# The first work of a hybrid decoder block: value projection of the undilated heads ahead of the state-space inputs, on raw x

## The chip, the cores and the metric

The kernel runs on one core of a Trainium2 chip. The metric is the device time of one execution in microseconds. The shapes are one batch of 512 tokens by 1024 model channels, in float32.

## The reference, cut to what matters

One decoder layer:

- `h = RMSNorm(x)`: every token's row is divided by its root mean square, and every channel is multiplied by `norm_w`.
- `proj = h @ w_in`, whose columns are split into `u` and `z` of a state-space branch (1024 columns each), queries, keys and values of three head groups (512 columns each per group), a gate `z_a` (512) and two merge gates `r_s`, `r_a` (1024 each).
- State-space branch: with `lam`, `dt`, `b` a diagonal complex recurrence over the tokens is run for 64 groups of 16 channels with 64 states, and read out with `c`; then GELU, a gated unit with `w_glu`, a SiLU gate and `w_ssm_out`.
- Attention branch: three head groups with window and dilation (128, 1), (512, 4) and (2048, 16). The values of the first group, which is not dilated, are the ones that this change moves. Then a SiLU gate and `w_attn_out`.
- The branches are gated, summed, multiplied by `w_o` and added to x.

Since the root mean square is one number per token, a projection can be made of raw x times `norm_w`, and its rows be divided by the root afterwards.

## The kernel before, in words

Every float32 product is made of three passes of a reduced float32 type: both operands are split into a high part (ScalarE, a copy that rounds) and a low part (VectorE, the difference), and TensorE adds high x high, high x low and low x high. So each weight block of 128x1024 costs one `w_hi` instruction on ScalarE (line 248) and one `w_lo` on VectorE (line 250), and `h` is split in the same way into `hT_hi` (line 349) and `hT_lo` (line 351), held transposed: channels on partitions, in eight slices k of 128, tokens along the free side.

A projection is made in one of two ways. Channel-major (`cm_unit`): 128 columns of the weights are the stationary side and all 512 tokens stream, 24 products (8 slices by 3 passes) of 512 columns. Token-major (`wide_granule`): 128 tokens of `h` are stationary and 512 columns of the weights stream, 96 products for 512 columns.

TensorE's instructions stand in the order of the code: each is issued behind the one before (`pe`, `follow`). In the first part of the kernel ScalarE's and VectorE's are pinned too, by `on_act` and `on_dve`. What goes through neither, as all work of GpSimd and the loads on SyncE's queue, is put in order by a planner when the program is built, by its own estimate of when each instruction can start. The engines and queues then work in that order and wait where an input is late.

The start: x is loaded in three parts (tokens are dealt so that row r of `x_all` holds tokens r, r+4, ...), with weights between them. TensorE warms up with 38 transposes of a unit matrix. The first half (rows 0 and 1) is squared and summed on ScalarE and VectorE (`square`, `square_dve`), `inverse_rms` makes the inverse root `rst`, `scale_dve` and `scale_act` multiply x by it in place, and `h_turn` turns the 16 blocks of 128x128 on TensorE into PSUM (`hps`). `h_split` multiplies by `norm_w` (`nwc`) and splits. `first_pass` then makes u0, u1 and u2, the first 384 channels of `u`, over the first 256 tokens, while the second half of x goes the same way; then over the second 256 tokens.

Behind it the coefficients of the recurrence are made from `lam` and `dt` on VectorE, with two sines on ScalarE (`sincos`); `f_turn` turns them on TensorE (`ftp`). The projections u3 to u7, `z_a`, `z`, `r_s`, the undilated values (`v0_granule`, 96 products) and a granule with other values follow as filler units. Events, given in blocks of six products of these units, hang the state-space work between them: `W0` the first input coefficients (`wps`), `K0B` the first output kernels, `Y0` the first read-out (`yps`). The recurrence itself (`step`, lines 753 to 758) runs on VectorE beside them. `d_load` loads the skip weights and multiplies them on GpSimd (line 812).

The values go through ScalarE (`act.copy`) into `vt` and from there to memory (`vd`), from which `v0_load` brings them back in the order of the attention.

## Time and profile before

| | |
|---|---|
| time, median of 3 runs | 668.4 us (668.23 to 668.57) |
| profiled execution, its own time | 668.63 us |
| its span | 666.7 us |
| TensorE busy | 660.2 us, 4617 products and transposes |
| VectorE busy | 466.2 us |
| ScalarE busy | 321.0 us |
| GpSimd busy | 116.8 us |
| granted TensorE clock over the span | 1.0 |

PE is TensorE, PEld its weight load, DVE VectorE, ACT ScalarE, POOL GpSimd, SP SyncE; a q behind a name is the engine's queue of issues. A row of the timeline gives start, length, engine, line, operation, out<-in, shapes and a count, and in brackets the idle time of the engine before it and what ended that. A row of the groups gives busy time, mean ns of one, and the idle time of the engine before. A row of the chain of waits gives start, length and what the end of the kernel hung on then. Products are pipelined, so their own lengths overlap; the distance between starts is what one costs.

### The profile page before, as it was taken

What the parts mean: (1) busy time and instruction counts of PE and PEld (TensorE: products, weight loads), DVE (VectorE), ACT (ScalarE), POOL (GpSimd) and SP (SyncE); (2) the same over time, 40 slices, a digit from 0 to 9 for tenths busy, and PEclk for the clock granted to TensorE, in tenths of its full rate; (3) what the DMA queues carried; (4) which work ended last, traced back from release to release, by engine and by line L of the source; (5) the groups of instructions that cost most, each with busy time, mean ns of one, the idle gap of its engine ahead of it and who ended that gap; (6) DMA issues with size and microseconds to landing.
All of it is one profiled execution on the core that took longest, in us unless ns stands there. A gap on an engine that the chain in (4) does not pass through costs nothing.

```text
span 666.7 us, 12357 instructions
## 1 busy us (share of the span) xinstructions
PE 660.2 (99%) x4617; PEld 553.7 (83%) x4617; DVE 466.2 (70%) x965; ACT 321.0 (48%) x676; POOL 116.8 (18%) x274
## 2 busy tenths in 40 slices
PE   8999999999999999999999999999999999999998
PEld 7988888888888888888888888888888888888887
DVE  7898989999786469833238676758575957657531
ACT  6636444432667545422444664557356645633210
POOL 1010000600375257600000030022002200210000
PEclk9999999999999999999999999999999999999999
DMA  9646364744666644564244223222232314347231
GB/s 310 128 126 178 85 189 132 183 140 130 169 151 154 156 139 142 165 207 118 64 126 128 80 63 112 64 77 83 80 94 64 96 50 126 104 139 277 94 127 63
DMA packets 137618, 85.25 MB, mean 128 GB/s; under 512 B 33104, under 2 KB 124248, under 8 KB 137304
## 3 DMA queue, kind: packets, MB, share of 16 engines
q1 hardware_dynamic: 135352, 81.98, 41.6%
q0 software_dynamic: 2048, 2.36, 2.4%
q8 instruction: 36, 0.59, 0.4%
q14 instruction: 22, 0.18, 0.1%
q10 hardware_dynamic: 160, 0.14, 0.1%
HBM read 70.03 MB, written 12.06 MB: 123 GB/s over the span
## 4 chain that ended last, share of the span: by engine, by line
PE 96%; DVE 1%; DMA 1%; issue 1%; ACT 0%; ACTq 0%
PE pj L69 81%; PE sps L69 3%; PE yps L69 3%; PE ot L69 2%; PE ptp L74 2%; PE qtp L74 2%; PE xps L69 1%; PE wps L74 1%; DMA x_all<-in_x_dram 1%; PE kps L69 1%; PE yT L74 1%; ACT w_hi L248 0%; DVE hT_lo L351 0%; PE hps L74 0%; PE cps L74 0%
## 5 line engine op out<-in xcount | busy, mean ns | idle before, releaser
L248 ACT ACTIVATE w_hi<-w_raw 128x1024 fp32r<-128x1024 f32 x94 | 99.3, 1059 | 169.1 <-PE pj L69 121.2
L250 DVE TENSOR_TENSOR w_lo<-w_raw,w_hi 128x1024 fp32r<-128x1024 f32 x94 | 118.9, 1266 | 66.0 <-ACT w_hi L248 65.5
L69 PE MATMUL pj<-hT_hi,w_hi 128*128 128x512 f32 (+1 forms) x312 | 119.0, 383 | 0.0
L69 PE MATMUL pj<-hT_lo,w_hi 128*128 128x512 f32 (+1 forms) x312 | 116.3, 375 | 0.4 <-DVE hT_lo L351 0.4
L69 PE MATMUL pj<-w_hi,hT_hi 128*128 128x512 f32 x288 | 115.2, 400 | 0.0
L69 PE MATMUL pj<-hT_hi,w_lo 128*128 128x512 f32 (+1 forms) x312 | 114.4, 374 | 0.0
L69 PE MATMUL pj<-w_hi,hT_lo 128*128 128x512 f32 x288 | 112.4, 390 | 0.0
L69 PE MATMUL pj<-w_lo,hT_hi 128*128 128x512 f32 x288 | 112.3, 390 | 0.0
L69 PEld LDWEIGHTS pj<-hT_hi,w_hi 128*128 128x128 f32 x312 | 59.1, 189 | 9.7
L69 PEld LDWEIGHTS pj<-hT_lo,w_hi 128*128 128x128 f32 x312 | 58.9, 189 | 9.9 <-DVE hT_lo L351 0.6
L69 PEld LDWEIGHTS pj<-hT_hi,w_lo 128*128 128x128 f32 x312 | 57.7, 188 | 10.7
L69 PEld LDWEIGHTS pj<-w_hi,hT_lo 128*128 128x128 f32 x288 | 54.0, 188 | 11.7
L69 PEld LDWEIGHTS pj<-w_hi,hT_hi 128*128 128x128 f32 x288 | 54.1, 188 | 10.5
L69 PEld LDWEIGHTS pj<-w_lo,hT_hi 128*128 128x128 f32 x288 | 54.2, 188 | 10.0
L1122 POOL COPY sw<-st 32x4 f32<-32x4 f32 x64 | 13.0, 202 | 177.3 <-ACT Pt L1078 174.8
L1023 DVE SCALAR_TENSOR_TENSOR qkp<-qtp,wcol,qkp 128x512 fp32r<-128x512 f32 (+1 forms) x32 | 23.5, 748 | 24.0 <-ACT qkp L1022 23.9
L1078 ACT ACTIVATE Pt<-Pt,st 128x256 f32<-128x256 f32 (+1 forms) x64 | 30.9, 484 | 19.2 <-DVE st L1076 19.2
L1022 ACT ACTIVATE qkp<-qtp,wcol 128x512 fp32r<-128x512 f32 (+1 forms) x32 | 21.2, 683 | 34.7 <-PE qtp L74 31.3
L848 POOL DMA_DIRECT2D dd<-kt x64 | 33.7, 536 | 2.3 <-POOL kt L844 2.1
L69 PE MATMUL pj<-w_lo,mT_hi 128*128 128x512 f32 (+1 forms) x72 | 26.3, 366 | 0.0
L69 PE MATMUL pj<-w_hi,mT_hi 128*128 128x512 f32 (+1 forms) x72 | 26.3, 366 | 0.0
L69 PE MATMUL pj<-w_hi,mT_lo 128*128 128x512 f32 (+1 forms) x72 | 26.3, 365 | 0.0
(298 smaller groups left out, 1172.0 us busy)
## 6 DMA issues: line engine op xcount, KB each, us to landing
w_raw<-in_w_in_dram SPq DMA_DIRECT2D x36, 512.0 KB
w_raw<-in_w_in_dram SPq DMA_DIRECT2D x128, 128.0 KB
w_raw<-in_w_glu_dram SPq DMA_DIRECT2D x8, 512.0 KB
w_raw<-in_w_ssm_out_dram SPq DMA_DIRECT2D x8, 512.0 KB
w_raw<-in_w_o_dram SPq DMA_DIRECT2D x8, 512.0 KB
w_early<-in_w_in_dram SPq DMA_DIRECT2D x4, 512.0 KB
ud<-uT SPq DMA_DIRECT2D x8, 256.0 KB
gd<-z SPq DMA_DIRECT2D x8, 256.0 KB
```

The source lines that it names most:

```text
L69: last[0] = nc.tensor.matmul(*a, **k)
L74: last[0] = nc.tensor.transpose(*a, **k)
L248: last_act[0] = act.activation(hi, raw, AF.Copy).ins
L250: dve.tensor_tensor(lo, raw, hi.bitcast(F32), op=ALU.subtract)
L848: pool.dma_start(M[Q * t:Q * t + Q, :, 0:P - Q * t], kt[:, :, t:].rearrange("q g k p -> q g (k p)"))
L1022: act.activation(hi, ps[sl], AF.Copy, scale=w)
L1023: dve.scalar_tensor_tensor(lo, ps[sl], w, hi.bitcast(F32), op0=ALU.mult, op1=ALU.subtract)
L1078: act.activation(o, o, AF.Exp, bias=nm, scale=-1.0, accum_out=st[:, kind, 1, h, b:b + 1])
L1122: pool.tensor_copy(sw[32 * r:32 * r + 32, :, :, b], st[32 * b:32 * b + 32, 1, :, :, r])
```

## The change

The first work of TensorE becomes the undilated values, token-major. The first half of x is turned as it lands, without scaling, times `norm_w`; the four weight chunks of the values (2 slices of k each) are multiplied with it slice by slice (`first_products`). The copies out of PSUM (`first_out`) multiply the rows of that half by `rst`. The second half of x is scaled before it is turned, as before. The first half is then scaled in place on GpSimd, turned a second time and split again, since all other projections need the scaled `h`. u0 to u2 become filler units like the rest; the values are no longer one of these. The loads at the start are reordered: half of x, three chunks of value weights (the first in two loads), the other half of x, the fourth chunk. The warm-up is 16 transposes, the turn of `norm_w`, and 6 more. The table turn moves from block 5 to block 3 of the filler units, `W0`, `K0B` and `Y0` by 2, 2 and 3 blocks; there are now 12 more blocks of `u` ahead of the rest and 16 fewer of values. The sines are queued behind the split of the second half (`hi_done`) and no longer behind the copy of u0.

```diff
-    WARM = 38
+    WARM = 16, 6
...
+    plan += wide_spec(w_in, (V0, 512))
     for c in range(KT):
         plan.append(cm_spec(w_in, U0 + c * P))
...
-    warming(WARM)
+    warming(WARM[0])
     nps = bank("nps")
     pe.transpose(nps[:, 0:KT], nw8, ident[:KT, :KT])
+    warming(WARM[1])
...
-    sp.dma_start(x_all[:, 0:2], x[0].rearrange("(i r) d -> i r d", r=NB)[:, 0:2])
-    fetch_w(0)
-    for r in (2, 3):
-        sp.dma_start(x_t[r], xv[r])
-        fetch_w(r - 1, w_early[:, 0] if r == 3 else None)
+    sp.dma_start(x_all[:, 0:2], xh[0])
+    raws_in[0] = wp.tile([P, 2, 512], F32, name="w_raw", tag="w_raw", bufs=2)
+    for k in range(2):
+        sp.dma_start(raws_in[0][:, k], plan[0][0][0][k * P:(k + 1) * P])
+    fetch_w(1)
+    fetch_w(2, wide_early[:, 0])
+    sp.dma_start(x_all[:, 2:4], xh[1])
+    fetch_w(3, wide_early[:, 1])
...
+    def first_products(i, h):
         hi, lo = loaded[i]
+        for k in range(2):
+            kk = 2 * i + k
+            for rs in ((2 * h,), (2 * h + 1,)) if kk else ((2 * h, 2 * h + 1),):
+                for th, w in ((hT_hi, hi), (hT_lo, hi), (hT_hi, lo)):
+                    for r in rs:
+                        pe.matmul(first_ps[r], th[:, kk, r * P:(r + 1) * P], w[:, k], start=kk == 0 and w is hi and th is hT_hi,
+                                  stop=kk == KT - 1 and w is lo, skip_group_check=True)
+
+    def first_out(r):
+        vt = t2k("vt")
+        on_act(lambda: act.activation(vt, first_ps[r], AF.Copy, **({"scale": rst[:, r:r + 1]} if r < 2 else {})))
+        sp.dma_start(vd[r], vt)
...
+    on_dve(lambda: dve.tensor_copy(nwc, nps[:, 0:KT]))
+    hps = turn_room(5)
+    h_turn(0, hps, range(6))
+    high, low = split_parts(0)
+    for k in range(2):
+        h_high(0, hps, k)
+        high(k)
+        h_low(0, hps, k)
+        low(k)
+    first_products(0, 0)
+    h_turn(0, hps, range(6, KT))
+    for i, ks in ((1, (2, 3)), (2, (4, 5))):
+        high, low = split_parts(i)
+        for k in range(2):
+            h_high(0, hps, ks[k])
+            h_low(0, hps, ks[k])
+            high(k)
+            low(k)
+        first_products(i, 0)
+    for kk in (6, 7):
+        h_high(0, hps, kk)
+        h_low(0, hps, kk)
+    square(2)
+    square_dve(3)
+    high, low = split_parts(3, spare)
+    inverse_rms(1)
+    scale_dve(3, 0, half)
+    scale_dve(3, half, D)
+    scaled = last_dve[0]
+    for k in range(2):
+        high(k)
+        low(k)
+    scale_act(2)
+    first_products(3, 0)
     square(0)
     square_dve(1)
     inverse_rms(0)
...
+    first_ps.append(bank("pj"))
+    hps = turn_room(4)
+    h_turn(1, hps, range(KT))
+    for kk in range(KT):
+        h_high(1, hps, kk)
+        h_low(1, hps, kk)
     hi_done = last_act[0]
+    for r in range(2):
+        pool.tensor_scalar(x_t[r], x_t[r], rst[:, r:r + 1], None, op0=ALU.mult)
+    first_out(0)
+    first_out(1)
+    first_products(0, 1)
+    first_products(1, 1)
+    dealt["g"] += 1
+    hps = turn_room(4)
+    h_turn(0, hps, range(KT))
+    for kk in range(KT):
+        h_high(0, hps, kk)
+        h_low(0, hps, kk)
+    first_products(2, 1)
+    first_products(3, 1)
+    taken[0] = 4
+    for i in range(2):
+        fetch_w(4 + i, w_early[:, 2 + i])
...
-    W0, K0B, V0B, Y0 = 16, 49, 74, 88
+    W0, K0B, Y0 = 14, 47, 85
...
+    prefetch(6)
+    first_out(2)
+    first_out(3)
...
-        with queued_after(copied[0]):
+        with queued_after(hi_done):
...
-    def v0_granule(at=()):
-        pss = beside_scan(at)
-        for r in range(NB):
-            vt = t2k("vt")
-            act.copy(vt, pss[r])
-            sp.dma_start(vd[r], vt)
...
-    events = [(3, begin_x), (6, lambda: early.update({3: load_u(3, sza[:, 3])})), (5, f_turn)]
+    events = [(3, begin_x), (3, f_turn)]
+    events += [(4 * j + 6, lambda j=j: early.update({j: load_u(j, sza[:, j])})) for j in range(4)]
...
-    events += [(V0B + 10, lambda: v0_load(0, V)), (Y0 - 10, lambda: load_us(0)), (Y0 - 10, lambda: load_us(1))]
+    events += [(Y0 - 4, lambda: v0_load(0, V)), (Y0 - 10, lambda: load_us(0)), (Y0 - 10, lambda: load_us(1))]
...
-    for kind, c in [("u", j) for j in range(3, 8)] + order:
-        n = 16 if kind in ("v0", "v") else 4
+    for kind, c in [("u", j) for j in range(8)] + order:
+        n = 16 if kind == "v" else 4
```

## The prediction

> **What bounds the kernel now.** I read the page's totals first, then the chain of waits, then the start of the timeline.

> ```profile
> span 666.7 us, 12357 instructions
> PE 660.2 (99%) x4617; PEld 553.7 (83%) x4617; DVE 466.2 (70%) x965; ACT 321.0 (48%) x676; POOL 116.8 (18%) x274
> ```

> TensorE is busy 660.2 of 666.7 us. The order of its instructions is fixed by the code, so a change can only move time by adding or removing TensorE work, or by changing its idle time, which can hardly sum to more than some us. The chain of waits (start, length, what) shows where that idle time lies.

> ```profile
> 0.75 5.07 DMA x_all<-in_x_dram
> ...
> 8.70 0.88 DVE x_all L332 x2
> ...
> 12.67 6.90 PE pj L69 x53
> 19.57 1.75 PE hps L74 x16
> 21.32 16.43 PE pj L69 x110
> 37.74 0.58 PE ftp L69 x16
> 38.33 15.19 PE pj L69 x66
> 53.52 1.24 PE wps L74 x8
> ```

> Until 12.67 the chain runs through the DMA of x, the root mean square and the scaling of x. From 12.67 it is TensorE alone. From there to the table turn (ftp, 37.74) lie 25.07 us. How many products those are, the groups by form say (all from 5 to 38 us), and the timeline says when the first turn of x began:

> ```profile
> L69 PE MATMUL pj<-hT_lo,w_hi 128*128 128x256 f32 x48 | 13.4, 291 | 0.4 <-DVE hT_lo L351 0.4
> L69 PE MATMUL pj<-hT_hi,w_hi 128*128 128x256 f32 x48 | 13.1, 286 | 0.0
> L69 PE MATMUL pj<-hT_hi,w_lo 128*128 128x256 f32 x48 | 11.3, 284 | 0.0
> 8.84 1.97 PE L74 MATMUL hps<-ident,x_all 128*128 128x128 f32 x16 [1.17 <-DVE x_all L332]
> ```

> There are 144 half-wide products (256 columns) for u0 to u2. Twelve of them stand before 12.67. In the 25.07 us stand the other 132, 16 transposes (1.75 us) and 30 full-wide products. A full-wide one costs 15.19/66 = 0.230 us. So 132 half-wide ones took 25.07 - 1.75 - 6.90 = 16.42 us, 0.124 each: more than half of 0.230. TensorE time lost before 12.67 is 12.67 - 12 x 0.124 - 1.75 = 9.43 us.

> **The change, part by part.**

> *Form.* The 144 half-wide products become 72 full-wide ones, since u0 to u2 now run over all 512 columns: 144 x 0.124 - 72 x 0.230 = 1.3 us gained. The 96 products of the values are full-wide before and after; they only move from the middle to the start.

> *Second turn.* 16 more transposes, as many as the 1.75 us row: 1.75 us lost.

> *Start.* Raw x goes to the transposes as soon as it lands, without square, root and scaling. The warm-up shrinks from 38 to 16 + 6 transposes. Their spacing is read in two stretches of the timeline:

> ```profile
> 3.11 1.67 PE L74 MATMUL warm<-ident 128*128 128x128 f32 x7
> 5.28 2.24 PE L74 MATMUL warm<-ident 128*128 128x128 f32 x19
> ```

> About 0.21 us each at first, 0.11 later. With 22 of them TensorE is through at about 5.6, just before x lands at 0.75 + 5.07 = 5.82. A gap of 0.3 us stands against the 1.17 us gap of before, behind which the transposes still ran at 0.11, so I cost it at nothing.
> [...]

> From the landing I step through the queues, which the code pins.

> ```profile
> 7.38 1.13 ACT L227 ACTIVATE w_hi<-w_raw 128x512 fp32r<-128x512 f32 x2
> 9.57 0.68 DVE L224 TENSOR_TENSOR w_lo<-w_raw,w_hi 128x512 fp32r<-128x512 f32 x1
> 9.75 2.45 ACT L349 ACTIVATE hT_hi<-hps,nwc 128x256 fp32r<-128x256 f32 x6 [0.62 <-PE hps L74]
> 12.14 2.05 DVE L351 SCALAR_TENSOR_TENSOR hT_lo<-hps,nwc,hT_hi 128x256 fp32r<-128x256 f32 x5
> 15.64 1.22 DVE L315 CUSTOM_DVE_ANT_0 junk<-x_all 128x1024 f32<-128x1024 f32 x1
> 18.08 1.15 ACT L328 ACTIVATE x_all<-x_all,scr 128x1024 f32<-128x1024 f32 x1 [0.82 <-DVE scr L324]
> 18.08 0.88 DVE L332 TENSOR_SCALAR x_all<-x_all,scr 128x512 f32<-128x512 f32 x2
> ```

> First transposes at 5.9; first high part of h 6.5 to 6.9 (0.41 each); high part of the weights to 7.5 (1.13/2 = 0.57); first product at 7.55. One slice k costs ScalarE 0.41 + 0.57 = 0.98, VectorE 2.05/5 + 0.68 = 1.09 at most, and TensorE 6 x 0.23 = 1.38. So TensorE is the bound for six slices: 7.55 + 6 x 1.38 + 4 transposes 0.44 = 16.3.

> The last two slices wait. VectorE must first end six slices (6.95 + 6 x 1.05 = 13.2), two more low parts (0.8), the square of row 3 (1.22, to 15.2), the root and reciprocal (16.86 to 18.08 in the rows above, 1.2), the scaling (0.88) and then the low part of the weights (0.68): 18.0, and 17.8 to 18.3 by the looser and tighter pace. TensorE has by then done two products of slice 6 and idles from 16.75 to 18.05. Ten products later, at 20.35, the first half is done. TensorE time lost: 20.35 - 48 x 0.23 - 16 x 0.109 = 7.6 us against 9.43: 1.8 gained.

> Do the loads keep up? The second half of x stands behind 2.6 MB. The rates of before in 40 slices of 0.625 us:

> ```profile
> GB/s 0 0 84 132 236 328 406 436 276 347 402 433 358 341 358 438 415 322 348 317 338 340 347 348 344 347 345 180 115 37 57 131 24 59 120 62 68 98 25 30
> ```

> Added up, 1.05 MB are moved by 5.1 us (the chain has the landing of x at 5.82, so 0.7 more to the signal), 3.67 MB by 12.3 and 4.2 MB by 13.8. So x's second half is there at 13.0, and VectorE, the later of the two engines, comes to its square at 14.0; the fourth weights are there at 14.5, needed at 15.4. Hidden, with 0.9 to 1.0 us of cover.

> *The scaling of rows 0 and 1 on GpSimd* (two 128x1024) is not in the trace. Nearest rows:

> ```profile
> L907 POOL MEMSET dd<- 128x1024 f32 x3 | 2.9, 951 | 44.2 <-DVE ab L419 36.5 <-DVE dd L575 7.7
> L121 POOL TENSOR_TENSOR aT<-at,aT 128x512 fp32r<-128x512 f32 x3 | 3.9, 1287 | 52.7 <-ACT aT L119 52.7
> ```

> From 0.95 (a fill of that size) to 2.6 us each (twice a two-input operation of half the size); I take 1.8, nearer to the one-input side. Its input is ready when VectorE has squared row 1 (18.6 to 19.8) and the root is taken (1.1): 20.9. So it ends between 22.8 and 26.1. TensorE asks for it after 16 transposes and 24 products: 20.35 + 1.75 + 5.5 = 27.6. Hidden by 1.5 us at worst, if GpSimd's queue is free (first rival).

> *Table turn.* It moves from the 30th to the 18th full-wide product of the u units, so TensorE reaches it at 7.6 + 114 x 0.23 + 48 x 0.109 = 39.0, not 37.74. Before, VectorE was ready only just in time:

> ```profile
> 16.87:37.31 20.44, 20.44 (x148) 19.33 (x147) 18.36 (x78) 13.26 (x21) 1.39 (x3) 1.00 0.58 113
> 32.92 1.28 ACT L505 ACT_TABLE_LOAD   x1
> 37.09 0.22 DVE L543 TENSOR_TENSOR pw<-scr 64x64 f32<-64x64 f32 x1
> ```

> (columns: stretch, length, busy TensorE, weight load, VectorE, ScalarE, GpSimd.) VectorE was busy 18.36 of 20.44 us. Between 18.0 and the turn it now has the eight low parts of the repeated turn (3.3 us), one square (1.22) and one low part of weights (0.6) more; it has one or two weight splits of 1.22 fewer, one scaling (0.88) and one square's root part fewer, and the sines no longer wait for the copy of u0 (2 us earlier). I get the tables at 38 to 39.5: a stall of 0 to 0.5, I take 0.2.

> *Copies and stores of the values* (four each) move from the middle to 24 to 37 us on ScalarE and SyncE; ScalarE was busy 13.26 of 20.44 there, and the next user of their banks is u1, at 40 us or later. Nothing.

> *Scan.* Its start comes one block (1.38 us) later against the state products, and two to three gates' VectorE work (0.68 each) falls into it.

> ```profile
> 161.65 0.69 DVE L758 TENSOR_TENSOR Xs<-Xs,scn 128x512 f32<-128x512 f32 x1
> ...
> 169.54 2.17 PE yps L69 x96
> ```

> The scan ended at 162.34, 7.2 us early; 7.2 - 1.4 - 2.0 leaves 3.8. Nothing.

> **Sum:** 1.8 + 1.3 - 1.75 - 0.2 = 1.15 us gained, up to 2.2 if VectorE keeps the tighter pace and the full-wide products run nearer 0.227, down to 0.2 with late tables. The profiled execution took 668.63 us (span 666.7 and 1.9 around it), 0.2 above the median 668.4; from the median this gives 667.2, and I put 667.0, as the half-wide products of the first stretch were the slower ones.

> **Rivals.**

> *GpSimd's queue is not free (slower).* The scaling of rows 0 and 1 is not pinned; the planner places it. In its queue stand three small products that wait for loads of the skip weights:

> ```profile
> 24.45 0.45 POOL L812 TENSOR_TENSOR dg<-dg,ident 16x128 f32<-16x128 f32 x1 [21.63 <-DMA dg<-in_d_skip_dram]
> 28.37 0.48 POOL L812 TENSOR_TENSOR dg<-dg,ident 16x128 f32<-16x128 f32 x1 [3.46 <-DMA dg<-in_d_skip_dram]
> 32.87 0.45 POOL L812 TENSOR_TENSOR dg<-dg,ident 16x128 f32<-16x128 f32 x1 [4.02 <-DMA dg<-in_d_skip_dram]
> ```

> If the planner believes that these loads land before 20.9, they stand ahead, and the second turn waits. For it: the planner's SyncE order shows that it expected quick landings.

> ```profile
> 29.40 0.63 SPq L431 DMA_DIRECT2D ud<-uT  x1
> 34.07 0.60 SPq L405 DMA_DIRECT2D sza<-ud  x1
> 34.77 1.84 SPq L431 DMA_DIRECT2D ud<-uT  x2
> ```

> The reload of u0 was put ahead of the second store, and the chip held the queue 4 us for it. Against it: some 6 MB are queued ahead, and the scaling comes earlier in the program. Price: 24.9 + 3.6 - 27.6 = 0.9 us with one ahead, 28.8 + 3.6 - 27.6 = 4.8 with two, 33.3 + 3.6 - 27.6 = 9.3 with three: 668.1, 672.0, 676.5. It decides from 23.9 us on, as the start of the scaling.
> [...]

> *Tables late.* If VectorE takes the weight splits of u0 to u2 (3 x 1.22) ahead of the tables, they are ready at 41 and TensorE idles 2 us: 669.0. For it: VectorE was nearly full there; against it: the sines start earlier.
> [...]

> *No real gain at the start.* If slices 6 and 7 cost as much as the scaling did before (lost time 9.4 instead of 7.6), 1.3 - 1.75 is a loss of 0.4: 668.8. Against it: the first product comes 1.7 us behind the landing of x, where now a scaling alone ends at 9.58.

> **How the numbers follow.** About 0.2% (1.3 us) is what a measurement here tells from no change. Forecast case (666.0 to 668.0): 0.60, of which 0.37 is faster and 0.23 same. GpSimd queue: 0.24, of it 0.05 same and 0.19 slower. Tables late: 0.09, of it 0.01 faster, 0.04 same and 0.04 slower. No gain at the start: 0.07, same 0.04, slower 0.03. Sums: 0.38, 0.36, 0.26. The range 665.9 to 672.5 leaves out three waiting loads above and about 4 in 100 below; the forecast's own range is 666.0 to 668.0.

> **What would show it.** First product of the values near 7.55; one TensorE gap of about 1.3 us near 17, ended by the weights' low part; no gap ahead of the second turn near 27.6 and GpSimd's scaling done by 26; at most 0.5 us ahead of ftp at 39; 512-wide products alone from u0 on. A gap behind GpSimd's x_all near 28, or ftp after 40, would make the prediction wrong.

## The result, and the profile after

The changed kernel takes 675.14 us (median of 4 runs, 674.78 to 675.73); the kernel before took 668.43 beside it. The ratio is 1.0103, with a 95% interval from 1.0091 to 1.0115: slower by 1%, where 667.0 was forecast. The profiled execution took 675.03 us, with a span of 673.3 against 666.7.

The totals of the changed kernel's page:

```profile
span 673.3 us, 12231 instructions
PE 662.2 (98%) x4545; PEld 551.4 (82%) x4545; DVE 468.0 (70%) x973; ACT 323.9 (48%) x686; POOL 123.2 (18%) x276
```

TensorE has 72 instructions fewer and is yet busy 2.0 us longer (662.2 against 660.2); the idle rest of the span grew from 6.5 to 11.1. So some work ran slower than before, and some waits are new. The chain of waits (start, length, what) shows where:

```profile
6.76 1.31 PE hps L74 x12
8.07 3.01 PE pj L69 x12
...
18.59 0.48 DVE x_all L335
19.07 0.61 DVE spare L225
19.73 4.14 PE pj L69 x10
23.87 1.11 PE hps L74 x10
...
44.94 0.23 DVE pw L580
45.21 0.54 PE ftp L69 x12
45.75 15.19 PE pj L69 x66
```

Ten products took 4.14 us from 19.73 on, where 66 of the same kind take 15.19 further down: 0.41 each against 0.23. The table turn (ftp) follows VectorE's last table (pw) and its last twelve transposes stand at 45.21 (the first four ran at 44.53), where the prediction had 39.0 and a stall of 0.2.

The waits of TensorE (who waited, for whom, us in total, how often, the longest):

```profile
PE xps L69 <- DMA Uj<-ud: 2.0, 1, 2.0
...
PE pj L69 <- DVE spare L225: 1.1, 1, 1.1
PE ftp L69 <- DVE scr L578: 1.0, 1, 1.0
PE pj L69 <- ACT spare L222: 0.9, 1, 0.9
PE hps L74 <- DVE scr L519: 0.7, 1, 0.7
PE ftp L69 <- DVE pw L580: 0.4, 1, 0.4
```

The row left out is the wait for the identity matrix at the very start, 1.6 us, as in the kernel before. The others are six waits, 6.1 us in all: two at slice 6 of the first half (spare), one at the second turn (hps), two at the table turn, and one at the state products (xps), for a reload of u7. The next three stretches are as long as the steps of the granted clock. Columns: stretch, length, busy time of TensorE, weight load, VectorE, ScalarE, GpSimd, then the granted clock, the DMA share and GB/s.

```profile
16.48:19.89 3.41, 1.45 (x6) 0.59 (x5) 3.02 (x11) 2.82 (x5) 0.00 (x0) 1.00 0.75 75
19.89:23.30 3.41, 3.41 (x9) 2.65 (x10) 3.38 (x22) 0.89 (x3) 0.00 (x0) 0.50 0.95 151
23.30:26.72 3.42, 3.42 (x24) 2.83 (x23) 1.43 (x6) 1.72 (x5) 0.74 (x2) 1.00 0.57 150
```

In the first TensorE was busy 1.45 of 3.41 us; in the second it got half the clock for exactly one such stretch, which I estimate to cost 3.41/2 = 1.7 us of work; in the third the clock is back. The ten slow products stand in that half clock: 4.14 us is 1.8 more than ten at 0.23.

What is late ahead of them is on ScalarE and VectorE. ScalarE's timeline (start, length, instruction, idle time before it):

```profile
9.14 0.64 ACT L222 ACTIVATE w_hi<-w_raw 128x512 fp32r<-128x512 f32 x1
11.34 0.47 ACT L350 ACTIVATE hT_hi<-hps,nwc 128x256 fp32r<-128x256 f32 x1 [1.56 <-PE hps L74]
```

ScalarE stood idle 1.56 us ahead of the split of slice 3. That slice had been turned with the first twelve transposes, but slice 6 lies in the other half of the same PSUM bank, and its transposes are among the four that TensorE does only after twelve products (10.9 to 11.3).

GpSimd's and then VectorE's timeline:

```profile
25.98 0.45 POOL L838 TENSOR_TENSOR dg<-dg,ident 16x128 f32<-16x128 f32 x1 [23.16 <-DMA dg<-in_d_skip_dram]
26.41 5.67 POOL L423 TENSOR_SCALAR x_all<-x_all,scr 128x1024 f32<-128x1024 f32 x2
32.05 1.95 POOL L838 TENSOR_TENSOR dg<-dg,ident 16x128 f32<-16x128 f32 x2
```

```profile
25.50 0.48 DVE L354 SCALAR_TENSOR_TENSOR hT_lo<-hps,nwc,hT_hi 128x256 fp32r<-128x256 f32 x1 [1.96 <-ACT hT_hi L350]
25.91 0.14 DVE L528 SCALAR_TENSOR_TENSOR scr<-scr 64x1 f32<-64x1 f32 x1
...
26.37 1.16 DVE L528 SCALAR_TENSOR_TENSOR scr<-scr 64x1 f32<-64x1 f32 x1
...
41.51 1.23 DVE L248 TENSOR_TENSOR w_lo<-w_raw,w_hi 128x1024 fp32r<-128x1024 f32 x1 [0.17 <-ACT w_hi L246]
```

One product for the skip weights stands ahead of the scaling of rows 0 and 1, and waits for its load. The two scalings take 5.67 us together. One and the same instruction of VectorE (L528, 64x1) takes 0.14 us ahead of that and 1.16 when the scaling has begun; two later ones beside the scaling (28.24 and 29.09) take 0.14 again.

The reload of u7 stands in the chain of waits further on:

```profile
100.18 4.79 DMA ud<-uT
104.98 4.18 DMA Uj<-ud
109.30 1.15 PE xps L69 x32
...
177.43 2.17 PE yps L69 x96
```

u7 is stored from 100.18, the reload goes at 104.98, when the store has landed, and 4.18 us later TensorE, which had asked at about 107.3, gets its data.

### The profile page after: what moved, and what is told of

It is laid out like the page before. It is cut to its first block, busy times and chain, and to the rows that moved or that the text cites. A ratio compares the mean times of both kernels' runs of the same rounds, so it can differ in the third digit from the quotient of the medians.

```text
span 673.3 us, 12231 instructions
## 1 busy us (share of the span) xinstructions
PE 662.2 (98%) x4545; PEld 551.4 (82%) x4545; DVE 468.0 (70%) x973; ACT 323.9 (48%) x686; POOL 123.2 (18%) x276
## 4 chain that ended last, share of the span: by engine, by line
PE 93%; DVE 3%; DMA 1%; ACT 1%; issue 0%; POOL 0%; ACTq 0%; POOLq 0%
PE pj L69 78%; PE sps L69 3%; PE yps L69 3%; PE ot L69 2%; PE ptp L74 2%; PE qtp L74 2%; PE xps L69 1%; PE wps L74 1%; DVE hT_lo L354 1%; DMA ud<-uT 1%; PE kps L69 1%; PE yT L74 1%; PE warm L74 1%; DMA Uj<-ud 1%; DVE w_lo L248 1%; PE hps L74 0%
## 5 line engine op out<-in xcount | busy, mean ns | idle before, releaser
L248 DVE TENSOR_TENSOR w_lo<-w_raw,w_hi 128x1024 fp32r<-128x1024 f32 x94 | 116.0, 1236 | 66.6 <-ACT w_hi L246 66.1
L69 PE MATMUL pj<-hT_hi,w_hi 128*128 128x512 f32 x288 | 115.3, 400 | 0.0
L69 PE MATMUL pj<-hT_hi,w_lo 128*128 128x512 f32 x288 | 112.5, 390 | 0.0
L69 PE MATMUL pj<-hT_lo,w_hi 128*128 128x512 f32 x288 | 112.4, 390 | 0.0
L69 PE MATMUL pj<-w_hi,hT_hi 128*128 128x512 f32 x280 | 112.3, 402 | 0.0
L69 PE MATMUL pj<-w_hi,hT_lo 128*128 128x512 f32 x280 | 109.1, 391 | 0.0
L69 PE MATMUL pj<-w_lo,hT_hi 128*128 128x512 f32 x280 | 109.1, 391 | 0.0
L69 PEld LDWEIGHTS pj<-hT_hi,w_lo 128*128 128x128 f32 x288 | 54.1, 188 | 11.6
L69 PEld LDWEIGHTS pj<-hT_hi,w_hi 128*128 128x128 f32 x288 | 54.5, 189 | 10.6
L69 PEld LDWEIGHTS pj<-hT_lo,w_hi 128*128 128x128 f32 x288 | 54.2, 188 | 10.2
L69 PEld LDWEIGHTS pj<-w_hi,hT_lo 128*128 128x128 f32 x280 | 52.5, 188 | 11.5 <-DVE scr L528 0.2
L69 PEld LDWEIGHTS pj<-w_hi,hT_hi 128*128 128x128 f32 x280 | 52.5, 188 | 10.3 <-ACT w_hi L222 0.2
L69 PEld LDWEIGHTS pj<-w_lo,hT_hi 128*128 128x128 f32 x280 | 52.8, 188 | 9.9 <-DVE w_lo L225 0.2
L1050 DVE SCALAR_TENSOR_TENSOR qkp<-qtp,wcol,qkp 128x512 fp32r<-128x512 f32 (+1 forms) x32 | 23.5, 747 | 24.0 <-ACT qkp L1049 23.9
L69 PE MATMUL pj<-w_lo,mT_hi 128*128 128x512 f32 (+1 forms) x72 | 26.4, 366 | 0.0
L69 PE MATMUL pj<-w_hi,mT_hi 128*128 128x512 f32 (+1 forms) x72 | 26.4, 366 | 0.0
L69 PE MATMUL pj<-w_hi,mT_lo 128*128 128x512 f32 (+1 forms) x72 | 26.3, 366 | 0.0
```

Source lines behind the costliest of these rows:

```text
L69: last[0] = nc.tensor.matmul(*a, **k)
L248: dve.tensor_tensor(lo, raw, hi.bitcast(F32), op=ALU.subtract)
L1050: dve.scalar_tensor_tensor(lo, ps[sl], w, hi.bitcast(F32), op0=ALU.mult, op1=ALU.subtract)
```

## The experiments

The theory after the trace: five independent things cost the time, a shared PSUM bank at the start, the clock behind it, the product ahead of GpSimd's scaling, the tables that VectorE has ready too late, and the reload of u7. The rival: there is one cause (a start that is 3.5 us late and moves everything behind it), and the other waits are its echo or hidden behind it. All ratios are against the kernel before. Five kernels alter one thing in the changed kernel, one alters the kernel before, and the last six put the remedies together and vary or take out one of them. All of them compute the reference's outputs in full.

**The reload of u7, two blocks later.** The state products of u6 and u7 are asked for two blocks later.

```diff
-    events += [(W0 + 5 + 6 * i, lambda i=i: x_pair(i)) for i in range(4)]
+    events += [(W0 + 5 + 6 * i + 2 * (i == 3), lambda i=i: x_pair(i)) for i in range(4)]
```

> One edit against the changed kernel: the last pair of state products (which reads u7 back from memory) two blocks, 2.8 us, later. Theory S (the stalls add up): the 2.0 us wait of TensorE on the reload of u7 near 107 is gone and nothing takes its place, so 673.1 us from 675.1, a gain of 2.0. Theory T (VectorE's tables alone set the time, all else only moves slack): the wait before the table turn is not touched and the late u7 was only cover; time within 0.5 us of 675.1.

Measured: 678.38 us (676.85 to 679.65), ratio 1.0147 (1.0130 to 1.0165). The wait for u7 is gone, and a longer one has come behind the scan:

```profile
PE kps L69 <- DVE ab L464: 2.9, 2, 2.4
```

The coefficients of the output kernel (ab) stand on VectorE behind the scan, and the scan now ends later. Behind that wait the clock was at half, from 183.0 to 186.4. It was also at half behind the table turn, where this edit changes nothing and the changed kernel's profile shows full speed behind the same two waits (1.0 and 0.4 us):

```profile
43.10:46.51 3.41, 2.02 (x21) 1.51 (x21) 2.39 (x12) 0.40 (x2) 0.00 (x0) 1.00 0.78 234
46.51:49.93 3.42, 3.42 (x10) 2.64 (x8) 3.36 (x6) 2.08 (x2) 0.95 (x1) 0.50 0.06 22
```

So some 1.7 of the 4.0 us between the two profiled spans (an estimate, half of 3.41) is not due to the edit. The two runs with a mean granted clock of 0.995, where the others have 0.992 (one fall of 3.41 us to half lowers the mean by 0.0025), took 676.85 and 677.67 us, still 1.7 to 2.5 more than the changed kernel: the wait was real, but moving its user alone moves the stall to a place where it costs more. The expected gain did not come; whatever is shifted at the state products must be shifted at the scan and the output kernel too.

**The PSUM banks.** Slices 6 and 7 go to the second halves of banks 0 and 1, whose slices have been split long before; slices 3 and 4 have banks of their own.

```diff
-    slots = {5: [(0, 0), (1, 0), (2, 0), (3, 0), (4, 0), (2, 1), (3, 1), (4, 1)], ...
+    slots = {5: [(0, 0), (1, 0), (2, 0), (3, 0), (4, 0), (2, 1), (0, 1), (1, 1)], ...
```

> One edit: slices 6 and 7 of the first turn share PSUM banks with slices 0 and 1 instead of 3 and 4, so the split of slice 3 need not wait until slice 6 has been turned. Expected for the part alone: ScalarE's wait of 1.56 us near 11 goes, VectorE reaches the square of row 3 about 1.1 us earlier (14.6 instead of 15.75), TensorE's two waits at slice 6 fall from 2.3 to about 1.3 us. Theory S: 1.1 us gained, and 1.6 more if the granted clock then stays at 1.0: 674.0 or 672.4. Theory T: VectorE gets to the tables at most 1.1 us earlier, so at most that: 674.0 to 675.1. A stall of 1.3 us that still drops the clock would speak against a threshold on idle time.

Measured: 675.45 us (675.05 to 676.55), ratio 1.0107 (1.0090 to 1.0124): no gain. ScalarE's timeline shows the split of slice 3 with no idle time, at 9.62 instead of 11.34, and TensorE's waits list shows where the gain went:

```profile
9.62 0.48 ACT L350 ACTIVATE hT_hi<-hps,nwc 128x256 fp32r<-128x256 f32 x1
```

```profile
PE hps L74 <- DVE w_lo L248: 2.5, 1, 2.5
...
PE hps L74 <- POOL x_all L423: 1.2, 1, 1.2
```

One of the two waits at slice 6 and the half clock behind them are gone (the ten products from 18.34 on took 2.59 us, not 4.14). But TensorE now reaches the second turn at 28.4, GpSimd's scaling ends at 32.4, 0.3 later than in the changed kernel, and the 3.7 us of waits there were followed by a half clock of their own: from 32.47 on 15 transposes took 2.55 us, where 16 take 1.75, and 18 products 5.06, where 18 at 0.23 take 4.1. Together that is 1.8 us over, about half of 3.41, and the mean granted clock of 0.997 is that of one fall. (The releaser named in the first row is inferred; row 1 of x, which GpSimd ends last, is what these transposes read.)

**Filling the waits.** Eight idle transposes go before the last turn of the first half, nine between the products of slice 6, into a PSUM bank whose first product comes later and overwrites them.

```diff
+    def fill(n):
+        for i in range(n):
+            pe.transpose(first_ps[3][:, 128 * (i % 4):128 * (i % 4) + 128], ident, ident)
...
+        if (i, h) == (3, 0):
+            fill(8)
...
+                    if (kk, h, rs, w is lo) == (6, 0, (0,), True):
+                        fill(9)
```

> One edit: 8 and 9 transposes of the unit matrix into an unused bank stand in TensorE's two waits at slice 6 (1.07 and 1.22 us long, 0.11 us each transpose), so that it is never idle there. Theory clock: the drop of the granted clock to 0.5 from 19.9 to 23.3 us comes from these waits; with them filled it stays 1.0, and the ten products behind them take 0.23 instead of 0.43 us each. Theory S: 1.7 us gained from that, 673.4. Theory T: the gain is taken back by the wait on GpSimd's scaling (it ends at 32.05 whatever TensorE does) and by the tables; 674.6 to 675.1, with TensorE's wait before the second turn grown from 0.9 to 2.5 us. If the clock drops all the same, something else than idle time drops it.

Measured: 675.24 us (673.58 to 677.37), ratio 1.0103 (1.0081 to 1.0124). With the waits at slice 6 filled the clock stayed full there (the mean granted clock of the profiled execution, 0.997, has room for one fall, and that one comes later), and TensorE was 2.2 us earlier (it began the next turn at 21.52 instead of 23.70), for nothing: it waited at the second turn (0.8 and 2.5 us), and the clock fell behind that (0.51 from 32.05 to 35.46). The two runs agree: what the start costs is real, but it is covered by GpSimd's lateness, and neither remedy is worth anything alone.

**GpSimd's queue.** The products of the skip weights are issued behind the scaling.

```diff
-        pool.tensor_scalar(x_t[r], x_t[r], rst[:, r:r + 1], None, op0=ALU.mult)
+        turned_x = pool.tensor_scalar(x_t[r], x_t[r], rst[:, r:r + 1], None, op0=ALU.mult).ins
...
-        pool.tensor_tensor(dg, dg, ident[0:Q, 0:Q].unsqueeze(1).broadcast_to([Q, 8, Q]), op=ALU.mult)
+        with tc.issue_after(turned_x):
+            pool.tensor_tensor(dg, dg, ident[0:Q, 0:Q].unsqueeze(1).broadcast_to([Q, 8, Q]), op=ALU.mult)
```

> One edit: the three small products of the skip weights are put behind the scaling of rows 0 and 1 in GpSimd's queue. The scaling can then start at 23.2, when the inverse root is there, instead of 26.4, and end near 29, 2 us before TensorE asks for it. Theory S: the wait of 0.9 us before the second turn goes, 674.2. Theory T: VectorE's tables come earlier only as far as the repeated split (eight low parts) starts earlier, so 0 to 0.9 gained: 674.2 to 675.1, and the wait before the table turn takes up what the other wait loses.

Measured: 673.70 us (671.91 to 673.87), ratio 1.0072 (1.0057 to 1.0087), 1.4 us less than the changed kernel. GpSimd's timeline:

```profile
22.99 5.69 POOL L423 TENSOR_SCALAR x_all<-x_all,scr 128x1024 f32<-128x1024 f32 x2 [20.17 <-PE hps L74]
```

The scaling started 3.4 us earlier and took as long as before, so its length isn't due to the queue; the wait at the second turn is gone. In the profiled execution the clock did not fall at slice 6, but behind the wait for u7 (columns as above):

```profile
104.10:107.50 3.40, 1.27 (x44) 1.16 (x39) 2.05 (x4) 1.31 (x6) 0.00 (x0) 1.00 0.79 210
107.50:110.95 3.45, 3.45 (x16) 2.67 (x13) 2.39 (x3) 1.07 (x6) 0.00 (x0) 0.51 0.31 83
```

The waits at slice 6 (0.9 and 1.1 us by the list in both kernels), behind which the clock fell in the changed kernel, were harmless here: they lie in two stretches, of which TensorE was busy 1.96 of 3.43 us (15.40 to 18.83) and 2.88 of 3.37 (18.83 to 22.20), and the granted clock was 1.00 in both.

**The kernel before, with fewer warm-up transposes.** If a stall of about 2 us is enough for the clock to fall, one can be made in a kernel that has none.

```diff
-    WARM = 38
+    WARM = 22
```

> The kernel before with one edit: 22 instead of 38 warm-up transposes, so TensorE is idle for about 3 us before the first turn at 8.84 instead of 1.2. Theory share (a stretch of 3.41 us with some 2 us or more of idle time in it halves the clock in the next 3.41 us, wherever the stretch begins): a drop to 0.5 for 3.4 us within the first 13 us in most executions, 0.5 to 1.5 us slower (part of it hidden behind VectorE there), and runs that spread by about 1 us. Theory whole (only a stretch wholly without work does it): no drop, 668.4.

Measured: 669.42 us (668.43 to 670.41, 10 runs), ratio 1.0015 (1.0005 to 1.0024). TensorE had finished the warm-up at 6.74 and got its first transposes at 8.94:

```profile
6.29:9.70 3.41, 1.21 (x11) 0.94 (x10) 3.01 (x12) 2.75 (x6) 0.00 (x0) 1.00 1.12 387
9.70:13.12 3.42, 3.42 (x19) 3.42 (x17) 2.60 (x7) 2.41 (x6) 0.00 (x0) 0.50 1.10 353
```

With 2.2 us idle in one stretch the next ran at half clock. It is the same sequence as at slice 6, in another kernel and with nothing else changed; the median is 1.0 us above the kernel before, and the runs spread over 2 us, so the profiled execution is one of several ways in which it goes. The one run with a mean granted clock of 1.0 took 668.43 us, as the kernel before.

**Blocks.** The table turn comes at block 5, where it stood before the change, and the state products, the scan and the outputs two blocks later.

```diff
-    W0, K0B, Y0 = 14, 47, 85
+    W0, K0B, Y0 = 16, 49, 87
...
-    events = [(3, begin_x), (3, f_turn)]
+    events = [(3, begin_x), (5, f_turn)]
```

> The changed kernel with the events of the state-space work two blocks later (table turn at block 5, W0 16, K0B 49, Y0 87), as far behind the start of u3 as in the kernel before. Theory S: the waits at the table turn (1.4 us) and on the reload of u7 (2.2 us) both go, as TensorE comes 2.8 us later to each, and the start is as in the changed kernel: 671.5 from 675.1, or 671.0 to 673.0 with the clock's drops at other places. A rival: the later W0 only moves the wait to the first read-out (scan), then 673 to 675.

Measured: 672.07 us (671.68 to 672.29), ratio 1.0053 (1.0038 to 1.0068): 3.1 us less than the changed kernel. Of the six waits the two at the table turn are gone and the one for u7 is 0.3. These waits' sum is 3.1 (1.4 + 2.0 - 0.3); the wait at the second turn grew by 0.4, so the waits alone give 2.7, and the profiled spans differ by 2.8. So the late tables and the late reload cost some 3 us, and are independent of the late start, which is still there.

**All of it.** Blocks, GpSimd's queue, banks and the nine transposes at slice 6 together.

> All repairs of single waits together: blocks of the run above, skip weights behind the scaling in GpSimd's queue, slices 6 and 7 in the banks of 0 and 1, and 9 transposes of the unit matrix in the wait ahead of slice 6's last pass. Theory S: against 675.1 the sum of 1.4 + 2.2 (blocks), 0.9 (GpSimd), 1.1 (banks) and 1.7 (clock) is 7.3, so 667.8, with no drop of the clock. That would also say that the change in itself is worth nothing measurable against 668.4. Theory T (VectorE sets the table turn): 1.0 to 1.5 us less of it, 669.0 to 669.5.

Measured: **667.35 us** (667.15 to 668.49, 10 runs), ratio 0.9987 (0.9977 to 0.9996). It beats both kernels, by 0.13% against the one before, which is less than the 0.2% taken above as the bound of what counts. Its waits list has one row, the wait for the identity matrix at the very start, which the kernel before has too:

```profile
PE warm L287 <- POOL ident masks.py:199: 1.6, 1, 1.6
```

```profile
22.07 5.69 POOL L431 TENSOR_SCALAR x_all<-x_all,scr 128x1024 f32<-128x1024 f32 x2 [19.25 <-PE hps L74]
```

```profile
20.96 1.75 PE hps L74 x16
...
28.43 1.75 PE hps L74 x16
...
42.43 0.58 PE ftp L69 x16
```

TensorE reaches the end of the first half at 20.96, GpSimd is through at 27.76, ahead of the second turn at 28.43, and nothing waits. The four remedies together take 7.8 us off the changed kernel.

**The scaling on ScalarE.** As the last kernel, but rows 0 and 1 are scaled on ScalarE, at 1.15 us each, and not on GpSimd.

```diff
+    scale_act(0)
+    scale_act(1)
...
-    for r in range(2):
-        pool.tensor_scalar(x_t[r], x_t[r], rst[:, r:r + 1], None, op0=ALU.mult)
```

> As the run above, but rows 0 and 1 are scaled on ScalarE (two of 1.15 us, pinned behind the inverse root, in the stretch in which it stood idle for 3.2 us) instead of on GpSimd (two of 2.85 us), and the skip weights' products stay where the planner puts them. Expected: VectorE's instructions of 1.2 us beside GpSimd's scaling (0.14 us otherwise) go, tables 1 to 2 us earlier; the split of the second half starts up to 0.5 us later. 0 to 0.5 us faster than the run above if the tables still bind, the same if not.

Measured: 669.69 us (668.99 to 670.53), ratio 1.0022 (1.0013 to 1.0032): slower by 2.3, not faster. VectorE's tables were ready 1.5 us earlier, with no GpSimd scaling beside them, but the two scalings stand on ScalarE ahead of the splits of the second half, and TensorE waits for those:

```profile
PE pj L69 <- ACT hT_hi L350: 1.7, 1, 1.7
```

```profile
22.20:25.63 3.43, 1.75 (x9) 1.23 (x8) 2.91 (x15) 3.43 (x8) 0.00 (x0) 1.00 0.79 186
25.63:29.04 3.41, 3.41 (x17) 2.81 (x16) 3.41 (x15) 3.08 (x6) 0.98 (x2) 1.00 0.60 168
```

Here 1.7 us idle in a stretch left the clock alone.

**Taking each remedy out again.** From the kernel with all of it (667.35), first without GpSimd's queue edit:

> The kernel with all repairs (667.35), but without the one of GpSimd's queue: one product of the skip weights stands ahead of the scaling again. TensorE now comes to the second turn near 28, the scaling ends near 32: a wait of 4 us in place of the 0.9 us of the changed kernel, since what had delayed TensorE ahead of it is gone. Theory share adds a drop of the clock by half for 3.4 us behind it, about 1.7 us. Part of it is taken back at the table turn, where 1 us of slack is. 670.5 to 672.5. Were the waits independent, 668.3.

Measured: 674.64 us (671.61 to 676.50), ratio 1.0092 (1.0062 to 1.0121): 7.3 us, more than expected.

```profile
PE hps L74 <- DVE scr L531: 2.5, 1, 2.5
PE hps L74 <- POOL x_all L431: 1.6, 1, 1.6
```

```profile
27.89:31.30 3.41, 1.43 (x6) 0.70 (x4) 3.41 (x6) 1.06 (x1) 3.41 (x2) 1.00 0.41 112
31.30:34.71 3.41, 1.25 (x6) 1.26 (x7) 3.41 (x13) 0.00 (x0) 3.09 (x3) 0.50 0.41 155
34.71:38.13 3.42, 3.42 (x15) 3.13 (x14) 1.98 (x8) 2.44 (x6) 0.00 (x0) 0.50 0.00 0
```

The waits fill the larger part of two stretches, and the clock was at half in the stretch behind each. That is 4.1 us of waits; for the clock I estimate up to 0.6 in the second stretch (half of the 1.25 us in which TensorE was busy) and 1.7 in the third. The profiled spans differ by 7.8; the rest, but for a wait of 0.4 for u7, I don't assign. The single runs say the same of the clock: the one with a mean granted clock of 0.999 took 671.61 us, 4.3 above the kernel with all of it and so the waits alone, and those with 0.997, 0.994 and 0.995 took 673.75, 675.52 and 676.50. The rival that the prediction named is thus dear; in the changed kernel the late start hid most of it.

Without the banks edit:

> The kernel with all repairs, but slices 6 and 7 of the first turn back in the banks of slices 3 and 4. ScalarE's wait of 1.56 us near 11 is back, VectorE's square and the scaling come about 1.1 us later, TensorE idles 1.1 us more at slice 6, no clock drop as less than 1.75 us of any stretch of 3.41 is idle: 668.4.

Measured: 669.08 us (668.53 to 669.68), ratio 1.0013 (1.0003 to 1.0022). The shared bank costs 1.7 us, near the 1.56 us that ScalarE waited there; TensorE's list shows it again as a wait of 0.9 us at slice 6, for the split on ScalarE.

Without the nine transposes:

> The kernel with all repairs, but without the nine transposes in the wait at slice 6. The wait left there is about 1.1 us. Theory share (a stretch of 3.41 us with under some 1.75 us idle does not drop the clock): no drop, 667.35 as with them. A theory by which any gap of about 1 us drops it: 1.5 us slower, 669.

Measured: 667.74 us (667.13 to 668.56), ratio 0.9992 (0.9982 to 1.0002). A wait of 0.9 us at slice 6 is back, and the clock stays (a mean of 1.0 in the profiled execution, and of 0.999 or 1.0 in every run). The difference of 0.4 us is within the intervals; with the banks mended, the fill is not needed.

Last, with all of it and a warm-up of 16 transposes without the six more, which end after x has landed:

```diff
-    WARM = 16, 6
+    WARM = 16, 0
```

> The kernel with all repairs, without the six transposes behind the turn of norm_w. They ended 0.75 us after x had landed in the profile, as the clock was still at half until 6.3. Expected: the first turn starts at 5.9, 0.3 to 0.7 us earlier, if ScalarE and VectorE behind it follow: 666.6 to 667.1. If the clock's rise depends on their work, it comes later and costs the same or more: 667.4 or above.

Measured: 667.42 us (667.04 to 668.95), ratio 0.9988 (0.9979 to 0.9998). The first turn starts at 5.85 instead of 6.61 in the profiled execution, and the median is the same. Between the two profiled executions 0.7 us of this is left at the table turn (41.74 instead of 42.43) and 0.5 at the end (spans of 665.4 and 665.9). But the runs of each kernel spread over more than that, and that of the kernel with all of it was above its median by 0.4; so a gain at the start is not shown, nor where it would be lost.

## Why the prediction was wrong

The whole difference can be laid out against the prediction's own steps, up to the table turn: 45.21 where it had 39.0 + 0.2, so 6.0 us late. The restart after slice 6 came at 19.73 and not 18.05: 1.7. The ten products behind it took 4.14 and not 2.3: 1.8. TensorE then idled 2.1 us up to the table turn (0.7 and 1.4 in the waits list) where 0.2 was foreseen: 1.9. Of the other 0.6, the first four products of the turn itself are 0.3; the rest lies in small pieces that I don't assign. The reload of u7 adds 2.0. That makes 8.0; the profiled executions differ by 6.4 where the sum had -1.15, which is 7.55, so 0.45 was won back in pieces that I don't assign either.

- *Form and second turn: right.* With every wait removed the kernel takes 667.35, where the sum of the parts was 667.2. This tests the sum as a whole, not each term, and it is in part luck: in that kernel the first half ended at 20.96 and not 20.35, and the table turn, 12 products later in the order, stood at 42.43 and not 39.0 + 2.8; most of these 0.6 us was won back further on, in pieces that I don't assign.
- *Start: the mechanism was right, a wait was left out.* The first product was foreseen at 7.55 and came at 8.07, as the warm-up ended late (at 6.75, not 5.6). The step that fails is VectorE's pace, "ends six slices at 13.2": it ended them at 15.05, and with other banks at 13.67. The step rested on rows of before, in which the splits follow each other without a wait. Here slices 3 and 6 share a PSUM bank, and ScalarE waited 1.56 us; the run with other banks and the run that takes them out again (1.7 us) show it.
- *The clock: the step that priced a stall of TensorE at its length alone is wrong.* The sum has no term for the clock. The traces show falls of 3.41 us, and one of twice that, behind stretches of 3.41 us in which TensorE was busy 1.45 (the changed kernel), 1.43 (all of it without the queue edit), 1.27 (the queue edit) and 1.21 us (the kernel before with fewer warm-up transposes); the clock didn't fall behind one in which it was busy 1.75 (the scaling on ScalarE; two stretches that do not fit an order by busy time are told at the end). So the wait at slice 6, foreseen in kind, was priced too low twice: its 1.3 us became 2.0 by the waits list, and then 1.7 more by the clock.
- *GpSimd's queue: the rival came true with one product ahead, at 0.7 us for the 0.9 it named.* But two of its inputs were off and cancelled. The scaling took 2.84 us each, beyond the upper bound of 2.6 and not 1.8; and TensorE came about 3.5 us later than foreseen. So its number was near by luck: on time, TensorE would have waited 4.1 us and, in the profiled execution, lost the clock twice (the run without the queue edit: 7.3 us).
- *Tables: the step "tables at 38 to 39.5" failed.* They were ready at 45.2. The trace shows three things that made them late. VectorE idled 1.96 us ahead of the splits of the second half, which came late with the first, and two of its small instructions beside GpSimd's scaling took 1.16 and 1.27 us, where their like took 0.14 and 0.19. And the rival's condition came true: VectorE took all three weight splits of u0 to u2 ahead of the tables, the one at 41.51 and these two.

```profile
32.48 1.21 DVE L248 TENSOR_TENSOR w_lo<-w_early,w_hi 128x1024 fp32r<-128x1024 f32 x1
...
34.70 1.21 DVE L248 TENSOR_TENSOR w_lo<-w_early,w_hi 128x1024 fp32r<-128x1024 f32 x1
```

  The run with all remedies separates the rival from the rest. There too the three splits stand ahead, but the start (0.6 us late) and the scaling are nearly in time, and the tables were ready at 41.3, where the rival had 41. Two blocks earlier TensorE would have stood at the turn at 39.7 (42.43 - 2.76), so I estimate a wait of 1.7 us by this alone. By difference, the other 3.9 us of the lateness came with the late start and the late scaling; how much each made was not separated. With the scaling on ScalarE the tables were 1.5 us earlier still.
- *The reload of u7: no step at all.* The prediction counted the copies and stores of the values, but not that the u units stand later against the state products: u7 is the last of them, its store and reload take 4.79 + 4.18 us, and the wait was 2.0. The instruction counts of the change showed nothing of it; the distance between producer and user in the order of blocks would have.
- *Scan: right.* Its last instruction ended at 173.6 (VectorE's timeline below), and the output products that follow start at 177.43 in the chain shown above, 3.8 us later, as worked out.

```profile
172.91 0.68 DVE L786 TENSOR_TENSOR Xs<-Xs,scn 128x512 f32<-128x512 f32 x1
```

  The run that delays u7's users shows what stands behind that margin: two blocks more and the coefficients are late.
- *Loads: right,* no wait for x or for weights up to the table turn is in the list.

The rival theory of a single late start is out: the blocks edit alone won 3.1 us with the start as late as ever. It holds in part for the second turn, where the late start hid what the product ahead of the scaling costs.

## What to carry to other kernels

When a change moves work from one end of a pinned order to another, list every producer whose distance to its user shrinks, loads and stores with their round trips included, and price each distance; here three of five losses (tables, u7, the second turn) were such distances. A remedy tried alone can show nothing because the next wait covers it: put all remedies together first, and then take each out again. A stall of TensorE of some 2 us I price, as an estimate, at nearly twice its length, as long as no trace shows the clock to hold: the 2.0 us at slice 6 were followed by a half clock that cost some 1.7 more. It held behind 1.7 us idle with the scaling on ScalarE, and in one trace even 1.4 us of waits (the table turn of the run that delays u7's users) was followed by such a fall of the clock.
